# Two-layer diffusion backbone on one core: a PSUM bank for the last of seven products, and GpSimd's instructions in pieces of 256 columns

## Chip, cores and metric

The kernel runs on one core of a Trainium2 chip. The metric is the device time of one execution in microseconds (us); the kernel before took 1140.18 us, the median of three runs (1138.74 to 1141.05).

## What is computed

512 latent tokens of 1024 channels pass through two layers. Each layer is a normalisation with modulation, a mixer (layer 0: differential attention beside a long convolution; layer 1: a pooling mixer), a second normalisation, and a squared-ReLU MLP of width 4096; a last RMSNorm ends it. What matters here is the MLP and the normalisation ahead of it:

```python
h_lat = h_lat + mod_l[5] * _sq_relu_mlp(
    _modulate(_rmsnorm(h_lat, norm2_g[i]), mod_l[3], mod_l[4]), mlp_w1[i], mlp_w2[i])

def _sq_relu_mlp(h, w1, w2):
    return jnp.square(jax.nn.relu(h @ w1)) @ w2
```

## The kernel before

Channels lie on the 128 partitions, tokens (512) on the columns. All products are float32 made of two rounded parts: an operand is split into a high part (`hi`, ScalarE's cast, L163) and a remainder (`lo`, a subtraction on VectorE or GpSimd, L164), and a product is three matmuls, hi·hi, hi·lo and lo·hi. A weight tile is 128x1024 (eight blocks of 128x128). It is fetched by SyncE, cast by ScalarE (1024 columns) and its remainder is formed by VectorE or, in most tiles, by GpSimd (`split`, called by `wload` and `w_split`).

The instructions of every engine stand in the order in which the code is written (`tc.manual_schedule`), so an engine whose next instruction waits does nothing else.

An MLP goes through four blocks of 1024 hidden channels: first the eight tiles `f` of the block (h @ w1, ReLU, square), then eight tiles `r` (times w2), each added into the stream `h` by VectorE (`h_add`, L1569). In layer 1 the first product of blocks 1, 2 and 3 is made for two tiles `f` and two token halves at once with **seven products** in place of eight (`pair7`, Strassen's scheme in Winograd's form): four pairs per block, three blocks, so twelve pairs of seven products. A product is 12 matmuls of 256 columns: eight with `whi` (L1669, L1670), then four with `wlo` (L1672). In a pair:

- `w0` and `w1` are prepared during the pair before, `w2` and `w3` at its start. They are sums of two weight tiles a and b: GpSimd adds a and b into `scr` (L1444) and folds b (L1447), and splits `w3` and the next `w0` (L164); VectorE forms the sums in `scr` for the next `w1` (`pair_sums`, L1430, L1431) and the remainders of `w1` and `w2` (L164).
- The products go to three PSUM banks of 512 columns, two halves each: `px`, `py`, `pz`, from a ring of six. The seven in order: `px` left, `py` left, `py` right, `pz` right, `px` right, `py` left again, `pz` left.
- VectorE adds them up: L1731 (both halves of `py` + `p1`, 512 columns), then `pair_sums` for the next pair, then `u3` (L1738, reads `px` right) and `s1` right (L1739, reads `pz` right), L1742, and at the end L1746 (both halves of `pz` + `u3`, 512 columns). The last product overwrites `pz` left, while L1739 reads `pz` right: TensorE waits for L1739 ahead of it.
- `finish` (L1754 to L1758) squares on ScalarE and forms the remainder `gl` on VectorE (L1758), interleaved with the next pair through `before(0)`, `before(1)`, and so on.

In block 0 of layer 1's MLP, `act_sums` forms the sums of the activations that the seven products read (`th`): GpSimd L1647, L1648 and L164, VectorE L1649 to L1653.

At the end of an MLP or mixing stage, `residual_norm` mixes the last tiles `r` with the next normalisation: squares (`ssq`, VectorE L1522 or GpSimd), column sums on TensorE (`nt`, L1530), and `mod` with its two VectorE steps L1543 and L1556 per tile.

Of the kernel before, what the change touches and what calls it, by code (L numbers as in the profile page):

```python
# [9 lines left out]
F32 = mybir.dt.float32  # L10
F32R = mybir.dt.float32r
AF = mybir.ActivationFunctionType
ALU = mybir.AluOpType
# [5 lines left out]
P = 128  # L19
D = 1024  # L20
ND = 8
T = 512
# [71 lines left out]
def body(ctx: ExitStack, tc: tile.TileContext, I, out):  # L94
# [6 lines left out]
    def f32(ap):  # L101
        return ap.bitcast(F32)
# [46 lines left out]
    def nm(s):  # L149
        cnt[0] += 1  # L150
        return f"{s}_{cnt[0]}"
# [7 lines left out]
    def w_tile(name, dt=F32R):  # L159
        return keep.tile([P, T], dt, name=nm(name), tag="W", bufs=8)  # L160

    def split(hi, lo, src, lo_eng=None):
        act.copy(out=hi, in_=src)  # L163
        (lo_eng or dve).tensor_tensor(out=lo, in0=src, in1=f32(hi), op=ALU.subtract)  # L164

    streams = {"s": (st, "s", 4, 2, st)}

# [1256 lines left out]
    def pair_sums(k):  # L1424

        if k in sums_done or k not in pairs:
            return
        sums_done.add(k)
        a, b, t = wraw[k], wraw[k + 1], scr[0]
        dve.tensor_tensor(out=t[:, :T], in0=b[:, :T], in1=a[:, :T], op=ALU.add)  # L1430
        dve.tensor_tensor(out=t[:, T : 2 * T], in0=t[:, :T], in1=a[:, T:], op=ALU.add)  # L1431

    def s3_part(k):
        c = (2 + k // 2 % 2) * T
        return scr[0][:, c : c + T]

    def pair_first(k, n=2):

        if k not in pairs:
            return  # L1440
        a, b = wraw[k], wraw[k + 1]
        if (k, 1) not in first_done:
            first_done.add((k, 1))
            pool.tensor_tensor(out=s3_part(k), in0=a[:, :T], in1=b[:, :T], op=ALU.add)  # L1444
        if n == 2 and (k, 2) not in first_done:
            first_done.add((k, 2))
            pool.tensor_tensor(out=b[:, :T], in0=b[:, :T], in1=b[:, T:], op=ALU.add)  # L1447

    def w_prep(n):
        while len(wsp) < min(n, len(wsrc)):  # L1450
# [182 lines left out]
    def mlp(layer, ah_, al_, nrm, i_norm, shift_in, last_norm, mod_next, load=None, seven=True):  # L1633
# [10 lines left out]
        def act_sums(i):  # L1644
            b1, b2, t = (ml.tile([P, T], F32, name=nm("b"), tag="sq", bufs=3) for _ in range(3))
            x, y = slice(0, 256), slice(256, 512)
            pool.tensor_tensor(out=b1, in0=f32(ah_[i]), in1=f32(al_[i]), op=ALU.add)  # L1647
            pool.tensor_tensor(out=b2, in0=f32(ah_[i + 4]), in1=f32(al_[i + 4]), op=ALU.add)  # L1648
            dve.tensor_tensor(out=t[:, x], in0=b1[:, x], in1=b1[:, y], op=ALU.subtract)  # L1649
            dve.tensor_tensor(out=t[:, y], in0=b2[:, y], in1=b1[:, y], op=ALU.subtract)  # L1650
            yield
            dve.scalar_tensor_tensor(out=b1[:, y], in0=t[:, y], scalar=-1.0, in1=b1[:, x], op0=ALU.mult, op1=ALU.subtract)
            dve.scalar_tensor_tensor(out=b2[:, y], in0=b1[:, y], scalar=-1.0, in1=b2[:, x], op0=ALU.mult, op1=ALU.subtract)  # L1653
            split(th[:, i, 0, 0:2, :], th[:, i, 1, 0:2, :], t.rearrange("p (a t) -> p a t", a=2), pool)
            split(th[:, i, 0, 2, :], th[:, i, 1, 2, :], b1[:, y], pool)
            split(ah_[i][:, y], al_[i][:, y], b2[:, y], pool)
            yield
# [8 lines left out]
        def product(o, w, c, b):  # L1666
            for i in range(4):
                l = w[0][:, c + i * P : c + (i + 1) * P]
                pe.matmul(o, l, b[i][0], start=(i == 0), stop=False)  # L1669
                pe.matmul(o, l, b[i][1], start=False, stop=False)  # L1670
            for i in range(4):
                pe.matmul(o, w[1][:, c + i * P : c + (i + 1) * P], b[i][0], start=False, stop=(i == 3))  # L1672
        for blk in range(4):
# [35 lines left out]
            def pair7(f, before):  # L1709

                k = wk[0]
                wk[0] += 2
                w_fetch(k + 8)
                pair_first(k + 2, 1)
                w0, w1 = wsp[k], wsp[k + 1]
                w2 = w_split(k, wraw[k + 1], dve)
                w3 = w_split(k + 1, s3_part(k), pool, T)
                pair_first(k + 2)
                x, y = slice(0, 256), slice(256, 512)
                px, py, pz = ps_m("f"), ps_m("f"), ps_m("f")  # L1720
                small = [ml.tile([P, 256], F32, name=nm("na"), tag="na", bufs=4) for _ in range(2)]
                p1, u3 = small
                s1 = ml.tile([P, T], F32, name=nm("r"), tag="r", bufs=3)
                twice = lambda v: v.rearrange("p (a t) -> p a t", a=1).to_broadcast([P, 2, 256])
                both = lambda v: v.rearrange("p (a t) -> p a t", a=2)
                product(px[:, x], w0, 0, b_part(0, 0))
                act.copy(out=p1, in_=px[:, x])
                product(py[:, x], w0, T, b_part(1, 0))
                before(0)
                product(py[:, y], w1, 0, t_part(2))  # L1730
                dve.tensor_tensor(out=both(s1), in0=both(py), in1=twice(p1), op=ALU.add)  # L1731
                before(1)
                w_prep(k + 3)
                before(4)
                pair_sums(k + 2)
                product(pz[:, y], w2, 0, t_part(0))
                product(px[:, y], w3, 0, t_part(1))
                dve.tensor_tensor(out=u3, in0=px[:, y], in1=s1[:, y], op=ALU.add)  # L1738
                dve.tensor_tensor(out=s1[:, y], in0=pz[:, y], in1=s1[:, y], op=ALU.add)  # L1739
                before(2)  # L1740
                product(py[:, x], w1, T, b_part(1, 1))
                dve.tensor_tensor(out=s1[:, y], in0=py[:, x], in1=s1[:, y], op=ALU.add)  # L1742
                w_prep(k + 4)
                product(pz[:, x], w2, T, [(ah_[i][:, y], al_[i][:, y]) for i in range(4)])
                s2 = ml.tile([P, T], F32, name=nm("r"), tag="r", bufs=3)
                dve.tensor_tensor(out=both(s2), in0=both(pz), in1=twice(u3), op=ALU.add)  # L1746
                for u in range(2):
                    mk = att_tile if f + u < 4 else w_tile
                    gh[f + u], gl[f + u] = mk("gh"), mk("gl")

                def finish(part):
                    for u, s, sign in ((0, s1, 1.0), (1, s2, -1.0)):
                        if part in (4 * u, 3):
                            act.activation(out=s, in_=s, func=AF.Relu, scale=sign)  # L1754
                            act.activation(out=gh[f + u], in_=s, func=AF.Square)
                            act.activation(out=s, in_=s, func=AF.Square)
                        if part in (u + 1, 3):
                            dve.tensor_tensor(out=gl[f + u], in0=s, in1=f32(gh[f + u]), op=ALU.subtract)  # L1758

                return finish  # L1760
# [64 lines left out]


    n1 = Norm()
    dh, dl = nl_tiles()
    sh1 = mods[:, 0, 3, :]
    w_fetch(6)  # L1830
# [321 lines left out]
```

## Time and profile before

| what | value |
|---|---|
| median of three runs | 1140.18 us |
| the profiled execution | 1138.79 us |
| its span | 1137.0 us |
| mean granted TensorE clock | 0.983 of full speed |
| TensorE busy (matmul) | 1084.9 us, 95% |
| VectorE busy | 772.9 us, 68% |
| GpSimd busy | 490.4 us, 43% |
| ScalarE busy | 482.4 us, 42% |

TensorE carries the kernel, so time is lost where it stands idle or where its clock is low. VectorE and GpSimd are far from full on average, but their busy time contains waiting: an instruction that has started and can't go on counts as busy.

### The profile page before, as it was taken

The numbers are of one execution on the slowest core, as the hardware profiler recorded it, in microseconds if no ns is written. First come the engines' busy times: TensorE is split into PE (matmuls) and PEld (weight loads), VectorE is DVE, ScalarE is ACT, GpSimd is POOL, SyncE is SP. The second block draws the span as 40 slices with busy tenths as digits, with TensorE's granted clock in tenths as the row PEclk, the third lists the DMA queues.
The fourth block names the chain that finished last, engine by engine and source line by source line (L and its number), as shares of the span: only waits on it lengthen the run. The fifth ranks groups of instructions, "written<-read, shape, count | busy, mean of one in ns | idle before, by whom it ended". The sixth has DMA issues, their size and how long they took to land.

```text
span 1137.0 us, 15915 instructions
## 1 busy us (share of the span) xinstructions
PE 1084.9 (95%) x6172; PEld 937.1 (82%) x6172; DVE 772.9 (68%) x1114; ACT 482.4 (42%) x812; POOL 490.4 (43%) x364
## 2 busy tenths in 40 slices
PE   8899999999999999999999999899997998999896
PEld 5488988788989988888888889898877888989886
DVE  6679899999856646686676683765457627725744
ACT  4454356666453531331341232655324614714541
POOL 4447337885564222122122123463476435354412
PEclk9899999999999999999999999999998999999998
DMA  9786753225522346567557462112322322332202
GB/s 328 276 271 214 251 170 128 75 65 168 180 100 75 111 137 236 166 205 256 168 197 252 147 213 97 40 73 74 111 75 75 109 78 74 112 111 75 94 19 74
DMA packets 48654, 161.42 MB, mean 142 GB/s; under 512 B 5250, under 2 KB 8578, under 8 KB 48452
## 3 DMA queue, kind: packets, MB, share of 16 engines
q1 hardware_dynamic: 46132, 149.93, 39.0%
q0 software_dynamic: 2448, 10.49, 2.7%
q8 instruction: 48, 0.79, 0.3%
q14 instruction: 26, 0.21, 0.1%
HBM read 156.20 MB, written 4.20 MB: 141 GB/s over the span
## 4 chain that ended last, share of the span: by engine, by line
PE 71%; DVE 16%; issue 3%; ACT 3%; POOL 3%; DMA 3%; SPq 0%; POOLq 0%; DVEq 0%; ACTq 0%
PE r L197 11%; PE r L199 10%; PE r L203 10%; PE f L199 6%; PE f L203 6%; PE f L197 6%; PE f L1669 2%; DVE g L629 2%; PE f L1672 2%; PE f L1670 2%; DVE gl L1758 1%; PE v L878 1%; DVE nl L1556 1%; DVE scr L1430 1%; DMA g<-in_adaN 1%
## 5 line engine op out<-in xcount | busy, mean ns | idle before, releaser
L164 POOL TENSOR_TENSOR wlo<-raw,whi 128x1024 fp32r<-128x1024 f32 x77 | 190.7, 2479 | 367.5 <-ACT whi L163 312.9
L197 PE MATMUL r<-gh,whi 128*128 128x512 f32 (+1 forms) x576 | 207.3, 368 | 0.0
L199 PE MATMUL r<-gl,whi 128*128 128x512 f32 (+1 forms) x576 | 207.0, 368 | 0.0
L163 ACT CAST whi<-raw 128x1024 fp32r<-128x1024 f32 x135 | 139.7, 1043 | 137.3 <-PE r L199 102.1
L1569 DVE SCALAR_TENSOR_TENSOR h<-r,mods,h 128x512 f32<-128x512 f32 (+1 forms) x81 | 54.3, 671 | 149.0 <-PE r L203 148.8
L203 PE MATMUL r<-gh,wlo 128*128 128x512 f32 (+1 forms) x576 | 130.7, 368 | 0.0
L197 PEld LDWEIGHTS r<-gh,whi 128*128 128x128 f32 x576 | 108.3, 188 | 19.1
L199 PEld LDWEIGHTS r<-gl,whi 128*128 128x128 f32 x576 | 108.4, 188 | 18.9
L203 PEld LDWEIGHTS r<-gh,wlo 128*128 128x128 f32 x576 | 100.5, 188 | 18.9
L197 PE MATMUL f<-nh,whi 128*128 128x512 f32 (+1 forms) x320 | 116.0, 370 | 0.0
L199 PE MATMUL f<-nl,whi 128*128 128x512 f32 (+1 forms) x320 | 116.0, 370 | 0.0
L1498 DVE CUSTOM_DVE_ANT_0 g<-g,sbcl 128x1024 f32<-128x1024 f32 x48 | 105.2, 2191 | 0.0
L164 DVE TENSOR_TENSOR wlo<-raw,whi 128x1024 fp32r<-128x1024 f32 x58 | 76.5, 1319 | 12.0 <-ACT whi L163 12.0
L1687 DVE TENSOR_TENSOR r<-r 128x512 f32<-128x512 f32 (+1 forms) x48 | 37.6, 784 | 67.9 <-ACT gh L1686 67.8
L1685 ACT ACTIVATE r<-f 128x512 f32<-128x512 f32 (+1 forms) x48 | 25.1, 523 | 131.6 <-PE f L203 130.0
L203 PE MATMUL f<-nh,wlo 128*128 128x512 f32 (+1 forms) x320 | 73.1, 371 | 0.0
L199 PEld LDWEIGHTS f<-nl,whi 128*128 128x128 f32 x320 | 60.2, 188 | 10.8
L197 PEld LDWEIGHTS f<-nh,whi 128*128 128x128 f32 x320 | 60.2, 188 | 10.8
L1669 PE MATMUL f<-nh,whi 128*128 128x256 f32 x192 | 50.8, 296 | 16.2 <-DVE r L1739 16.2
L203 PEld LDWEIGHTS f<-nh,wlo 128*128 128x128 f32 x320 | 56.3, 188 | 10.8
L197 PE MATMUL u<-ah,whi 128*128 128x512 f32 x160 | 63.3, 395 | 0.7 <-ACT vh L889 0.7
L199 PE MATMUL u<-al,whi 128*128 128x512 f32 x160 | 62.5, 391 | 0.0
(413 smaller groups left out, 2525.3 us busy)
## 6 DMA issues: line engine op xcount, KB each, us to landing
raw<-in_w SPq DMA_DIRECT2D x128, 512.0 KB, 4.4
g<-in_adaT SPq DMA_DIRECT2D x80, 512.0 KB, 4.2
g<-in_adaN SPq DMA_DIRECT2D x16, 512.0 KB, 8.5
raw<-in_w_hy SPq DMA_DIRECT2D x12, 512.0 KB, 4.4
raw<-in_w_qk SPq DMA_DIRECT2D x8, 512.0 KB, 4.0
pth<-in_pth POOLq DMA_DIRECT2D x4, 768.0 KB, 6.8
raw<-in_w_out SPq DMA_DIRECT2D x5, 512.0 KB, 4.0
x<-in_xT SPq DMA_DIRECT2D x8, 256.0 KB, 7.3
```

The lines of the kernel that those rows point to most:

```text
L163: act.copy(out=hi, in_=src)
L164: (lo_eng or dve).tensor_tensor(out=lo, in0=src, in1=f32(hi), op=ALU.subtract)
L197: pe.matmul(ps, wh[:, c], ah[i][:, t0 : t0 + n], start=(i == 0), stop=False)
L199: pe.matmul(ps, wh[:, c], al[i][:, t0 : t0 + n], start=False, stop=False)
L203: pe.matmul(ps, wl[:, i * P : (i + 1) * P], ah[i][:, t0 : t0 + n], start=False, stop=(i == k - 1))
L629: dve.tensor_tensor_reduce(out=g, in0=g, in1=sbc[0], scale=1.0, scalar=0.0, op0=ALU.mult, op1=ALU.add, accum_out=mods[:, 0, 2 + k // ND, k ...
L1498: dve.tensor_tensor_reduce(out=gin[k], in0=gin[k], in1=sbc[0], scale=1.0, scalar=0.0, op0=ALU.mult, op1=ALU.add, accum_out=mods[:, layer, ...
L1569: dve.scalar_tensor_tensor(out=hs[d][:, seg], in0=pp[:, :n], scalar=gate[:, d : d + 1], in1=hs[d][:, seg], op0=ALU.mult, op1=ALU.add)
L1669: pe.matmul(o, l, b[i][0], start=(i == 0), stop=False)
L1670: pe.matmul(o, l, b[i][1], start=False, stop=False)
L1685: act.activation(out=r, in_=pp[:, :n], func=AF.Relu)
L1687: dve.tensor_tensor(out=r, in0=r, in1=r, op=ALU.mult)
```

## The change

A flag `pieces` is set ahead of the last five tiles of layer 0's output projection, in front of the first MLP. From there GpSimd's remainders (`split` with GpSimd) go in slices of 256 columns: 1024 columns as four instructions, 512 as two. L1444 and L1447 go in two slices each, and the 512-column split of `th` in `act_sums` becomes two splits of 256 (ScalarE's cast too). The 512-column sums L1647 and L1648 stay whole.

In `pair7` the last product has a bank `pw_` of its own, the fourth of the pair in the ring of six. The two 512-column additions become two of 256 each (seven additions of 256 columns per pair, before two of 512 and three of 256), a third small tile `u2` joins `p1` and `u3`, and `pair_sums` moves behind `s1` right, `u3` and `s2` right on VectorE.

```diff
+    pieces = [False]
+
     def split(hi, lo, src, lo_eng=None):
         act.copy(out=hi, in_=src)
-        (lo_eng or dve).tensor_tensor(out=lo, in0=src, in1=f32(hi), op=ALU.subtract)
+        if lo_eng is pool and pieces[0]:
+
+            w = src.shape[-1]
+            for c in range(0, w, 256):
+                r = slice(c, min(c + 256, w))
+                pool.tensor_tensor(out=lo[:, r], in0=src[:, r], in1=f32(hi)[:, r], op=ALU.subtract)
+        else:
+            (lo_eng or dve).tensor_tensor(out=lo, in0=src, in1=f32(hi), op=ALU.subtract)
...
-            pool.tensor_tensor(out=s3_part(k), in0=a[:, :T], in1=b[:, :T], op=ALU.add)
+            for r in (slice(0, 256), slice(256, T)):
+                pool.tensor_tensor(out=s3_part(k)[:, r], in0=a[:, r], in1=b[:, r], op=ALU.add)
...
                 product(py[:, y], w1, 0, t_part(2))
-                dve.tensor_tensor(out=both(s1), in0=both(py), in1=twice(p1), op=ALU.add)
+                dve.tensor_tensor(out=s1[:, x], in0=py[:, x], in1=p1, op=ALU.add)
+                dve.tensor_tensor(out=u2, in0=py[:, y], in1=p1, op=ALU.add)
                 before(1)
                 w_prep(k + 3)
                 before(4)
+                product(pz[:, y], w2, 0, t_part(0))
+                dve.tensor_tensor(out=s1[:, y], in0=pz[:, y], in1=u2, op=ALU.add)
+                product(px[:, y], w3, 0, t_part(1))
+                dve.tensor_tensor(out=u3, in0=px[:, y], in1=u2, op=ALU.add)
+                s2 = ml.tile([P, T], F32, name=nm("r"), tag="r", bufs=3)
+                dve.tensor_tensor(out=s2[:, y], in0=pz[:, y], in1=u3, op=ALU.add)
                 pair_sums(k + 2)
-                product(pz[:, y], w2, 0, t_part(0))
-                product(px[:, y], w3, 0, t_part(1))
-                dve.tensor_tensor(out=u3, in0=px[:, y], in1=s1[:, y], op=ALU.add)
-                dve.tensor_tensor(out=s1[:, y], in0=pz[:, y], in1=s1[:, y], op=ALU.add)
                 before(2)
                 product(py[:, x], w1, T, b_part(1, 1))
                 dve.tensor_tensor(out=s1[:, y], in0=py[:, x], in1=s1[:, y], op=ALU.add)
                 w_prep(k + 4)
-                product(pz[:, x], w2, T, [(ah_[i][:, y], al_[i][:, y]) for i in range(4)])
-                s2 = ml.tile([P, T], F32, name=nm("r"), tag="r", bufs=3)
-                dve.tensor_tensor(out=both(s2), in0=both(pz), in1=twice(u3), op=ALU.add)
+                pw_ = ps_m("f")
+                product(pw_[:, x], w2, T, [(ah_[i][:, y], al_[i][:, y]) for i in range(4)])
+                dve.tensor_tensor(out=s2[:, x], in0=pw_[:, x], in1=u3, op=ALU.add)
...
     n1 = Norm()
+    pieces[0] = True
```

On TensorE, block 2's second pair, the end of the sixth product (into `py`) and the start of the seventh. Before, the seventh goes to `f_8885`, which is `pz`, and waits for VectorE:

```order
L1672 MATMUL f_8884<-nh_7055,wlo_8848 128x256
L1672 MATMUL f_8884<-nh_7056,wlo_8848 128x256
L1672 MATMUL f_8884<-nh_7057,wlo_8848 128x256
L1669 MATMUL f_8885<-nh_7050,whi_8874 128x256 [waits DVE_49]
L1670 MATMUL f_8885<-nl_7058,whi_8874 128x256
L1669 MATMUL f_8885<-nh_7051,whi_8874 128x256
```

Now it goes to `f_9228`, the new bank, and nothing is waited for:

```order
L1686 MATMUL f_9121<-nh_7190,wlo_9082 128x256
L1686 MATMUL f_9121<-nh_7191,wlo_9082 128x256
L1686 MATMUL f_9121<-nh_7192,wlo_9082 128x256
L1683 MATMUL f_9228<-nh_7185,whi_9109 128x256
L1684 MATMUL f_9228<-nl_7193,whi_9109 128x256
L1683 MATMUL f_9228<-nh_7186,whi_9109 128x256
```

The wait of TensorE's queue on VectorE ahead of the seventh product is gone. On VectorE, the same pair. Before:

```order
L1731 TENSOR_TENSOR r_8888<-f_8884,na_8886 128x512 [waits PE_49,Activation_49]
L1758 TENSOR_TENSOR gl_8866<-r_8763,gh_8865 128x512 [waits DVE_49,Activation_49]
L1430 TENSOR_TENSOR scr_7169<-raw_8710,raw_8676 128x512 [waits DMAHW5_49,DMAHW6_49,DVE_49,Pool_49]
L1431 TENSOR_TENSOR scr_7169<-scr_7169,raw_8676 128x512 [waits DVE_49]
L1738 TENSOR_TENSOR na_8887<-f_8883,r_8888 128x256 [waits PE_49]
L1739 TENSOR_TENSOR r_8888<-f_8885,r_8888 128x256 [waits DVE_49]
L1758 TENSOR_TENSOR gl_8868<-r_8863,gh_8867 128x512 [waits Activation_49]
L1742 TENSOR_TENSOR r_8888<-f_8884,r_8888 128x256 [waits DVE_49,PE_49]
L164 TENSOR_TENSOR wlo_8981<-scr_7169,whi_8980 128x1024 [waits Activation_49]
L1746 TENSOR_TENSOR r_8996<-f_8885,na_8887 128x512 [waits PE_49]
```

Now (L1439 and L1440 are `pair_sums`, L1772 is `gl`, L173 the remainder of the next `w1`):

```order
L1742 TENSOR_TENSOR r_9126<-f_9121,na_9123 128x256 [waits PE_49,Activation_49]
L1743 TENSOR_TENSOR na_9124<-f_9121,na_9123 128x256
L1772 TENSOR_TENSOR gl_9100<-r_8991,gh_9099 128x512 [waits DVE_49,Activation_49]
L1748 TENSOR_TENSOR r_9126<-f_9122,na_9124 128x256 [waits DVE_49,PE_49]
L1750 TENSOR_TENSOR na_9125<-f_9120,na_9124 128x256 [waits PE_49]
L1752 TENSOR_TENSOR r_9206<-f_9122,na_9125 128x256 [waits DVE_49]
L1439 TENSOR_TENSOR scr_7304<-raw_8934,raw_8895 128x512 [waits DMAHW6_49,DMAHW5_49,Pool_49]
L1440 TENSOR_TENSOR scr_7304<-scr_7304,raw_8895 128x512 [waits DVE_49]
L1772 TENSOR_TENSOR gl_9102<-r_9064,gh_9101 128x512 [waits Activation_49]
L1756 TENSOR_TENSOR r_9126<-f_9121,r_9126 128x256 [waits PE_49]
L173 TENSOR_TENSOR wlo_9225<-scr_7304,whi_9224 128x1024 [waits Activation_49]
L1760 TENSOR_TENSOR r_9206<-f_9228,na_9125 128x256 [waits PE_49]
```

The two instructions of `pair_sums` now stand behind the three additions that read PSUM, and so behind the fifth product of the pair.

## Rows read from the trace of the kernel before

**Rows 1.** The page, parts 1 and 5: busy us and share; a group's busy us, mean ns.
```profile
PE 1084.9 (95%) x6172; PEld 937.1 (82%) x6172; DVE 772.9 (68%) x1114; ACT 482.4 (42%) x812; POOL 490.4 (43%) x364
...
L163 ACT CAST whi<-raw 128x1024 fp32r<-128x1024 f32 x135 | 139.7, 1043 | 137.3 <-PE r L199 102.1
```
**Rows 2.** Waits: engine, line, awaited engine and line: us in total, times, longest.
```profile
PEld f L1669 <- DVE r L1739: 18.6, 12, 4.1
PE f L1669 <- DVE r L1739: 16.2, 9, 3.9
PE nt L1530 <- DVE ssq L1522: 3.8, 2, 2.5
```
**Rows 3.** Timeline, second pair of block 2: TensorE; columns start us, duration us, instruction, [idle before].
```profile
956.12 0.64 PE L1672 MATMUL f<-nh,wlo 128*128 128x256 f32 x4
...
961.79 0.63 PE L1672 MATMUL f<-th,wlo 128*128 128x256 f32 x4
963.21 0.64 PE L1672 MATMUL f<-nh,wlo 128*128 128x256 f32 x4
966.29 0.39 PE L1669 MATMUL f<-nh,whi 128*128 128x256 f32 x1 [2.44 <-DVE r L1739]
```
**Rows 4.** Timeline, the same pair: VectorE.
```profile
960.30 2.71 DVE L1758 TENSOR_TENSOR gl<-r,gh 128x512 fp32r<-128x512 f32 x1
962.94 1.77 DVE L1430 TENSOR_TENSOR scr<-raw,raw 128x512 f32<-128x512 f32 x1
964.75 0.69 DVE L1431 TENSOR_TENSOR scr<-scr,raw 128x512 f32<-128x512 f32 x1
965.36 0.42 DVE L1738 TENSOR_TENSOR na<-f,r 128x256 f32<-128x256 f32 x1
965.81 0.42 DVE L1739 TENSOR_TENSOR r<-f,r 128x256 f32<-128x256 f32 x1
...
967.08 1.22 DVE L164 TENSOR_TENSOR wlo<-scr,whi 128x1024 fp32r<-128x1024 f32 x1
```
**Rows 5.** Timeline, the same pair: GpSimd.
```profile
958.38 1.29 POOL L1447 TENSOR_TENSOR raw<-raw 128x512 f32<-128x512 f32 x1
960.05 2.42 POOL L164 TENSOR_TENSOR wlo<-raw,whi 128x1024 fp32r<-128x1024 f32 x1 [0.38 <-ACT whi L163]
962.43 1.73 POOL L1444 TENSOR_TENSOR scr<-raw,raw 128x512 f32<-128x512 f32 x1
```
**Rows 6.** Groups by line and shape, GpSimd: busy us, mean ns, idle before us.
```profile
L164 POOL TENSOR_TENSOR wlo<-raw,whi 128x1024 fp32r<-128x1024 f32 x77 | 190.7, 2479 | 367.5 <-ACT whi L163 312.9 <-PE r L203 54.6
```
**Rows 7.** Timeline, the kernel's end: three GpSimd instructions of 256 columns back to back.
```profile
1130.35 2.09 POOL L1974 TENSOR_TENSOR o<-hm,nbs 128x256 f32<-128x256 f32 x3 [1.23 <-ACT nbs L1969]
```
**Rows 8.** Windows: stretch, length, busy us of PE, PEld, DVE, ACT, POOL; granted clock, DMA, GB/s.
```profile
862.00:866.00 4.00, 3.02 (x14) 3.02 (x15) 2.50 (x6) 1.91 (x2) 0.00 (x0) 0.57 0.67 231
1057.00:1060.50 3.50, 3.50 (x19) 3.50 (x19) 2.40 (x3) 2.02 (x4) 1.90 (x1) 0.52 0.64 257
...
726.00:729.50 3.50, 3.50 (x18) 3.50 (x18) 0.60 (x3) 0.69 (x2) 0.70 (x1) 0.51 0.02 5
364.20:367.60 3.40, 3.40 (x18) 3.40 (x18) 0.65 (x2) 1.88 (x2) 2.52 (x2) 0.51 0.00 0
```
**Rows 9.** Timeline, end of layer 0's MLP: GpSimd, VectorE and TensorE.
```profile
716.83 2.24 DVE L1556 SCALAR_TENSOR_TENSOR nl<-na,mods,nh 128x256 fp32r<-128x256 f32 x1
...
720.12 0.47 DVE L1556 SCALAR_TENSOR_TENSOR nl<-na,mods,nh 128x256 fp32r<-128x256 f32 x1
...
721.34 2.36 POOL L164 TENSOR_TENSOR wlo<-raw,whi 128x1024 fp32r<-128x1024 f32 x1 [2.54 <-ACT whi L163]
721.70 2.27 DVE L1556 SCALAR_TENSOR_TENSOR nl<-na,mods,nh 128x256 fp32r<-128x256 f32 x1 [0.71 <-ACT nh L1551]
...
724.46 0.35 PE L1530 MATMUL nt<-sil,ssq 128*128 128x1 f32 x2 [2.52 <-DVE ssq L1522]
```
**Rows 10.** Timeline, start of block 1 of layer 1's MLP: TensorE.
```profile
851.43 0.38 PE L1669 MATMUL f<-th,whi 128*128 128x256 f32 x1 [2.18 <-ACT th L163]
```

More of the change, by code (lines that the diff above doesn't have):

```diff
@@ L1443, in pair_first @@
             first_done.add((k, 1))
-            pool.tensor_tensor(out=s3_part(k), in0=a[:, :T], in1=b[:, :T], op=ALU.add)
+            for r in (slice(0, 256), slice(256, T)):
+                pool.tensor_tensor(out=s3_part(k)[:, r], in0=a[:, r], in1=b[:, r], op=ALU.add)
         if n == 2 and (k, 2) not in first_done:
             first_done.add((k, 2))
-            pool.tensor_tensor(out=b[:, :T], in0=b[:, :T], in1=b[:, T:], op=ALU.add)
+            for c in (0, 256):
+                pool.tensor_tensor(
+                    out=b[:, c : c + 256], in0=b[:, c : c + 256], in1=b[:, T + c : T + c + 256], op=ALU.add
+                )
     def w_prep(n):
@@ L1653, in act_sums @@
             dve.scalar_tensor_tensor(out=b2[:, y], in0=b1[:, y], scalar=-1.0, in1=b2[:, x], op0=ALU.mult, op1=ALU.subtract)
-            split(th[:, i, 0, 0:2, :], th[:, i, 1, 0:2, :], t.rearrange("p (a t) -> p a t", a=2), pool)
+            for n in range(2):
+                split(th[:, i, 0, n, :], th[:, i, 1, n, :], t[:, n * 256 : (n + 1) * 256], pool)
             split(th[:, i, 0, 2, :], th[:, i, 1, 2, :], b1[:, y], pool)
@@ L1720, in pair7 @@
                 px, py, pz = ps_m("f"), ps_m("f"), ps_m("f")
-                small = [ml.tile([P, 256], F32, name=nm("na"), tag="na", bufs=4) for _ in range(2)]
-                p1, u3 = small
+                p1, u2, u3 = (ml.tile([P, 256], F32, name=nm("na"), tag="na", bufs=4) for _ in range(3))
                 s1 = ml.tile([P, T], F32, name=nm("r"), tag="r", bufs=3)
-                twice = lambda v: v.rearrange("p (a t) -> p a t", a=1).to_broadcast([P, 2, 256])
-                both = lambda v: v.rearrange("p (a t) -> p a t", a=2)
                 product(px[:, x], w0, 0, b_part(0, 0))
```

## The prediction

> **What bounds the kernel now.** I read the engines' busy time first: TensorE is busy 95% of the span, nobody else over 70% [rows 1], so what counts is where TensorE waits or runs slow. The list of waits comes next. From the start of the first MLP on, one entry stands out: the seventh product of a pair waits for VectorE's L1739, in all 16.2 us of idle matmul time and 18.6 us of idle weight loads, for twelve pairs [rows 2]. The second entry is 3.8 us ahead of the column sums of two normalisations [rows 2].
>
> The timeline of one pair shows why. The fifth product's last four matmuls run to 961.79 + 0.63 = 962.42 and the sixth's to 963.85; the seventh starts at 966.29 [rows 3]. VectorE has the additions L1738 and L1739, which need only the fifth product, behind three other instructions. The remainder `gl` takes 2.71 us, the first sum 1.77, the second 0.69, and L1739 ends at 966.23 [rows 4]. The same shape of instruction takes 0.69 us when nothing disturbs it [rows 4]. GpSimd tells the rest: its 1024-column remainder runs 960.05 to 962.47, and `gl`, begun at 960.30, ends at 963.01, 0.54 us after it. GpSimd's next, 512 columns, begun at 962.43, takes 1.73 where its like took 1.29, and ends 1.15 us after `gl`; the first sum, begun at 962.94, ends 0.55 us after that [rows 4, 5]. So the two engines take turns, instruction by instruction, in whatever reads two operands from SBUF, and the long one makes the short one wait. The additions from PSUM (L1738, 0.42) show no such wait. The Trainium skill says the same ("SBUF — State Buffer", Who interferes with whom: a VectorE instruction with two SBUF inputs and a GpSimd one that reads SBUF exclude each other for a whole instruction); the trace agrees, with 2.71 us for 0.69.
>
> The normalisation ahead of layer 1 shows it again: a VectorE step of 0.47 us takes 2.24 and 2.27 us, the second time beside a GpSimd remainder of 2.36 us that began 0.36 us earlier, and TensorE then waits 2.52 us for VectorE [rows 9].
>
> **The change part by part.** All terms are against the profiled execution, 1138.8 us; gains have a minus.
>
> *The bank.* The changed order has no wait ahead of the seventh product. The idle time there goes: between 16.2 and 18.6 us [rows 2]. Matmuls overlap a little where nothing waits, and that overlap returns too, so I take **-18**.
>
> *The clock after those waits.* After two of them the granted clock stood at its lower level, 1.2 GHz: 4.0 us at a mean of 0.57 and 3.5 us at 0.52 of full speed [rows 8], which is 4.0 x 0.43 + 3.5 x 0.48 = 3.4 us of lost speed, part of the first inside the wait itself. If TensorE no longer stops there, I expect no fall there: **-3.0** (0 to -3.4).
>
> *`pair_sums` moved back.* It feeds the next pair's `w1`, so the question is what is late next. Take the pair of the rows without TensorE's wait. Products end every (961.79 - 956.12)/4 = 1.42 us [rows 3], the seventh would follow the sixth at about 963.7, and the next pair's third product, the first user of `w1`, starts three later, at 963.7 + 3 x 1.42 = 967.9, and its low parts are needed at 968.9. The fifth product is done at 962.42; three additions of 0.42 bring VectorE to 963.8. Each sum now waits for at most one GpSimd piece, about 0.7, and takes 0.55 after it: 965.0 and 966.3. ScalarE's cast of 1.04 us [rows 1] gives the high part at 967.4, 0.5 us early. `gl` runs beside the cast, and VectorE's remainder of 1.22 us [rows 4] gives the low part at 968.7 to 969.4, from 0.2 early to 0.5 late. It fits, with little to spare.
>
> *The turns as a budget.* In one block GpSimd has 36 pieces (six each of L1444 and L1447, eight for `w3`, 16 for the 1024-column remainders), and VectorE eight remainders of 1024 and twelve instructions of 512 columns with two SBUF operands. A piece counts between 1.15/2 = 0.57 us (what 512 columns took after VectorE let go) and 0.73 (three in a row take 2.09, so 0.70 each, and the last of a row a little more [rows 7]). VectorE's count 1.22 and 0.55 to 0.69 [rows 4]. The sum is 36 x 0.57 + 9.8 + 6.6 = 36.9 us at the low end and 36 x 0.73 + 9.8 + 8.3 = 44.4 at the high one, against 28 x 1.42 = 39.8 us of products. So the cover is thin: nothing is lost at the low end, 4.6 us per block at the high one. I take the low end as the nearer, since the measured turns overlap at their ends, and put **+1.0 per block, +3** in all (0 to +13.8), for waits that appear at the next pair's weights and at the hand-over to the tiles `r`, where the last `gl` now ends later against TensorE.
>
> *GpSimd's own length.* 77 remainders of 1024 columns become four pieces each: 4 x 0.68 = 2.7 us for 2.4, and 40 instructions of 512 become two. That is some 30 us more GpSimd time in a span where it is 43% busy [rows 1]. Nearly all of it hides: those tiles are prepared two products `r` ahead, and GpSimd stands idle 368 us in front of them [rows 6]. If that cover were gone, it would cost TensorE 0.3 us per tile. It shows in one place, the start of block 1, where `act_sums` stands behind L1444, L1447 and a 1024-column remainder on GpSimd and TensorE then waits 2.18 us for `th` [rows 10]: **+0.8** (0.3 to 1.2). The two casts of `th` in place of one lie in that term.
>
> *VectorE's seven additions.* 7 x 0.42 against 2 x 0.69 + 3 x 0.42 is 0.3 us more per pair, in time that VectorE has; the fourth tile of the bank ring and the third small tile are released a pair earlier than they are asked for. Nothing.
>
> *The normalisations.* At the end of layer 0's mixing and of its MLP, two VectorE steps each stand 1.8 us too long behind a GpSimd remainder [rows 9]. In pieces each waits at most some 0.7, so VectorE is about 1.1 earlier twice over, 2.2 us in all, and of the 3.8 us of TensorE's wait [rows 2] (1.3 and 2.52) 1.2 and 2.1 go: **-3.3** (-2.0 to -3.8). After both, the clock was low for 3.5 us at 0.51 and 3.4 at 0.51 [rows 8], 1.7 us each. A short wait for ScalarE's square stays, so I count one of the two: **-1.7** (0 to -3.4).
>
> Sum: -18 - 3.0 + 3 + 0.8 - 3.3 - 1.7 = -22.2, so 1138.8 - 22.2 = 1116.6 us. The profiled execution lies 1.4 us under the median of the runs, at their lower edge (1138.74 to 1141.05), so I forecast **1117** for the median.
>
> **The rivals.**
> 1. *The turns are too many* (high end of the budget). The waits go from the seventh product to the next pair's first and third, at 4.6 us per block in place of 1.0. For it: the budget's high end passes the products, and `pair_sums` starts later. Against it: GpSimd's last pair in a block is light, and a measured turn is short. Time: 1117 + 3 x 3.6 = 1128.
> 2. *Slower: GpSimd's pieces set the pace.* Splitting doesn't lessen what the two engines must do one after the other, and each piece adds its own start. A block with seven products takes 39.8 + 16.2/3 = 45.2 us now. With h us per piece the budget is 36h + 18.1, and it passes 45.2 at h = 0.75, and eats the 5 us of the normalisations too above h = 0.80. The point that decides is a piece above 0.80 us. At h = 0.90 it is 50.5 us, 5.3 more per block, less 5: 1140 + 16 - 5 = 1151. Against it: alone, 256 columns take 0.70 [rows 7]. The rule of the Trainium skill named above ("SBUF — State Buffer", Who interferes with whom) speaks for this rival: whole instructions exclude each other, so by it alone pieces move waits about and make no room. The trace agrees with the exclusion in each turn above, with its 0.54 and 0.55 us.
> 3. *The bank is not the wait.* Then only the normalisations gain, 5 us less 0.8: 1136. Against it: the changed order shows the seventh product with no wait at all.
>
> **How the numbers follow.** Forecast 0.74, rival 1 0.17, rival 2 0.05, rival 3 0.04. The best bounds together give 1138.8 - 18.6 - 3.4 + 0.3 - 3.8 - 3.4 = 1110; upward the range takes in rival 1, to 1129. A measurement of this kernel tells 0.2% (2.3 us) from no change. Faster by more than that are the forecast, rival 1 and most of rival 3: 0.92; within it 0.03; slower 0.05.
>
> **What would show it.** Right: no wait on VectorE ahead of the seventh product; pairs of 9.9 us (7 x 1.42); no instruction of `gl` or of the sums above some 1.4 us; GpSimd's pieces at 0.7 to 0.85; full clock through blocks 2 and 3; TensorE's wait ahead of L1530 under 1 us. Rival 1 would show as waits on `whi` or `wlo` at the next pair's first, third or fourth product. The prediction is wrong if TensorE still waits over 5 us in the three blocks beyond the start of block 1, or if GpSimd's pieces run one after another while VectorE stands.

## The result and the profile after

| kernel | median (runs) | ratio to before, 95% interval |
|---|---|---|
| before | 1140.62 us (4: 1138.74 to 1143.05) | |
| changed | 1110.73 us (4: 1110.01 to 1111.55) | 0.974 [0.972, 0.976] |

The changed kernel is 29.9 us faster; 23 were forecast. The time lies in the range, near its fast end. Its profiled execution took 1111.55 us with a span of 1109.6, 27.4 us under the span before.

Page of the changed kernel, parts 1 and 5, which answers to [rows 1] and [rows 6]:

```profile
PE 1076.8 (97%) x6172; PEld 931.1 (84%) x6172; DVE 716.5 (65%) x1138; ACT 480.7 (43%) x816; POOL 581.1 (52%) x635
...
L171 POOL TENSOR_TENSOR wlo<-raw,whi 128x256 fp32r<-128x256 f32 x308 | 271.2, 913 | 296.1 <-ACT whi L165 257.0
```

GpSimd is 90.7 us busier and VectorE 56.4 us less, though VectorE has 24 instructions more: what VectorE lost was waiting inside its instructions. TensorE has the same number of matmuls and is busy 8.1 us less; a matmul at the low clock counts longer.

Waits of TensorE in the changed kernel (engine, line, awaited engine and line: us in total, times, longest), which answer to [rows 2]:

```profile
PE f L1683 <- ACT th L165: 2.3, 1, 2.3
...
PE nt L1543 <- ACT sq L1531: 1.7, 3, 0.9
...
PE f L1686 <- POOL wlo L171: 0.5, 1, 0.5
...
PE f L1683 <- ACT whi L165: 0.5, 1, 0.5
...
PE f L1684 <- POOL th L171: 0.4, 1, 0.4
PE nt L1543 <- DVE ssq L1535: 0.3, 1, 0.3
```

The entry of 16.2 us is gone, and the 3.8 us ahead of the column sums are 0.3. The largest entry left in the MLP is the wait for `th` at the start of block 1, 2.3 us, which was there before.

Timeline, second pair of block 2, VectorE in the changed kernel (start, duration, instruction), which answers to [rows 4]:

```profile
947.23 1.25 DVE L1439 TENSOR_TENSOR scr<-raw,raw 128x512 f32<-128x512 f32 x1
948.51 1.11 DVE L1440 TENSOR_TENSOR scr<-scr,raw 128x512 f32<-128x512 f32 x1
949.55 1.22 DVE L1772 TENSOR_TENSOR gl<-r,gh 128x512 fp32r<-128x512 f32 x1
950.69 0.41 DVE L1756 TENSOR_TENSOR r<-f,r 128x256 f32<-128x256 f32 x1
951.03 1.43 DVE L173 TENSOR_TENSOR wlo<-scr,whi 128x1024 fp32r<-128x1024 f32 x1
```

The same stretch, GpSimd, which answers to [rows 5]:

```profile
945.80 3.28 POOL L171 TENSOR_TENSOR wlo<-raw,whi 128x256 fp32r<-128x256 f32 x4
949.03 2.34 POOL L1454 TENSOR_TENSOR scr<-raw,raw 128x256 f32<-128x256 f32 x2
```

`gl` beside GpSimd takes 1.22 us where [rows 4] have 2.71; GpSimd's pieces take 3.28/4 = 0.82 and 2.34/2 = 1.17 each there, against 0.70 back to back [rows 7]. The engines still take turns, but what VectorE waits in one, 1.22 - 0.69 = 0.53 us, is now under the length of one 256-column piece. The sums and `gl` stay below the 1.4 us that the prediction set as their mark: in the three blocks the longest `gl` takes 1.27 us and the longest sum 1.25. GpSimd's pieces don't keep theirs, 0.7 to 0.85 us: the 308 of the page have a mean of 0.913, because they wait in the turns too.

Windows of the changed kernel (length, busy us of PE, PEld, DVE, ACT, POOL; granted clock, DMA share, GB/s): the place of the first clock fall of before [rows 8], the start of block 1, and blocks 2 and 3 of the seven products:

```profile
364.20:367.60 3.40, 3.40 (x31) 3.40 (x30) 2.86 (x7) 2.52 (x7) 3.40 (x5) 1.00 0.01 2
846.20:849.70 3.50, 3.34 (x15) 3.34 (x16) 2.49 (x3) 2.45 (x4) 3.50 (x5) 0.51 0.00 0
929.30:968.90 39.60, 39.60 (x337) 39.60 (x336) 31.60 (x48) 24.98 (x38) 32.05 (x34) 1.00 0.26 92
1013.20:1052.90 39.70, 39.70 (x337) 39.70 (x336) 31.59 (x48) 24.75 (x37) 31.57 (x34) 1.00 0.28 94
```

Blocks 2 and 3 run without any gap at 2.4 GHz. The clock stood at its lower level only once in the stretch from the first normalisation to the end of the MLP's blocks, behind the wait for `th`: the granted clock is 1.00 from 364.2 to 846.2 and from 849.7 to 1053.0.

The time by place, from the starts of the matmuls in the timelines. A block here runs from the start of its first product to the start of the matmul that follows its 28th. In the changed kernel block 2 goes from 929.23 to 968.98, before from 944.36 to 989.56.

| stretch | before | after | difference |
|---|---|---|---|
| all ahead of block 1's first pair | 845.40 | 838.77 | -6.63 |
| block 1 of seven products | 54.78 | 46.28 | -8.50 |
| block 2 | 45.20 | 39.75 | -5.45 |
| block 3 | 46.38 | 39.74 | -6.64 |

The four make 27.2 of the 27.4 us of the spans. The 6.6 us ahead of block 1 lie at the two normalisations: the same matmul starts at 359.85 before and 359.71 after ahead of the first, at 367.58 and 364.43 behind it, and at 729.32 and 722.48 behind the second. Their waits for VectorE fell by 3.8 - 0.3 = 3.5 us, and both clock falls of [rows 8] that followed them are gone, 1.7 us each, 3.4: together 6.9, with the 6.6 measured.

### The profile page after: what moved, and what is told of

It is laid out like the page before. It is cut to its first block, busy times and chain, and to the rows that moved or that the text cites. A ratio compares the mean times of both kernels' runs of the same rounds, so it can differ in the third digit from the quotient of the medians.

```text
span 1109.6 us, 16252 instructions
## 1 busy us (share of the span) xinstructions
PE 1076.8 (97%) x6172; PEld 931.1 (84%) x6172; DVE 716.5 (65%) x1138; ACT 480.7 (43%) x816; POOL 581.1 (52%) x635
## 5 line engine op out<-in xcount | busy, mean ns | idle before, releaser
L171 POOL TENSOR_TENSOR wlo<-raw,whi 128x256 fp32r<-128x256 f32 x308 | 271.2, 913 | 296.1 <-ACT whi L165 257.0
L1701 DVE TENSOR_TENSOR r<-r 128x512 f32<-128x512 f32 (+1 forms) x48 | 32.0, 667 | 81.2 <-ACT gh L1700 81.1
L173 DVE TENSOR_TENSOR wlo<-raw,whi 128x1024 fp32r<-128x1024 f32 x58 | 73.7, 1271 | 10.9 <-ACT whi L165 10.9
L1511 DVE CUSTOM_DVE_ANT_0 g<-g,sbcl 128x1024 f32<-128x1024 f32 x48 | 65.3, 1361 | 0.0
L734 POOL TENSOR_TENSOR wlo<-raw,whi 128x1024 fp32r<-128x1024 f32 x17 | 42.5, 2501 | 37.4 <-ACT whi L725 25.0
```

Of the source, the lines that this page charges most:

```text
L171: pool.tensor_tensor(out=lo[:, r], in0=src[:, r], in1=f32(hi)[:, r], op=ALU.subtract)
L734: ew(pool if k else dve).tensor_tensor(out=wts[k][1], in0=raws[k], in1=f32(wts[k][0]), op=ALU.subtract)
L1511: dve.tensor_tensor_reduce(out=gin[k], in0=gin[k], in1=sbc[0], scale=1.0, scalar=0.0, op0=ALU.mult, op1=ALU.add, accum_out=mods[:, layer, ...
```

## The experiments

Two things in the changed kernel could make it faster: what was done to the pairs (a bank and an order), and the pieces. The first four runs take them apart. All have the time of before from the same chip beside them: 1140.79 us in the first four, 1140.08 in the next four, 1140.05 and 1140.47 in the last two.

**Bank and order alone, GpSimd whole**

```diff
-    pieces[0] = True
...
-            for r in (slice(0, 256), slice(256, T)):
-                pool.tensor_tensor(out=s3_part(k)[:, r], in0=a[:, r], in1=b[:, r], op=ALU.add)
+            pool.tensor_tensor(out=s3_part(k), in0=a[:, :T], in1=b[:, :T], op=ALU.add)
```

(L1458 and the split of `th` likewise.)

> The bank of its own and the new order of VectorE's additions stay; GpSimd's instructions are whole again (1024 and 512 columns). Theory: in the pairs TensorE waits for nothing long even beside whole GpSimd instructions, because the additions it depends on stand ahead of the sums; the pieces earn their share at the two normalisations, 6.6 us between the two traces (TensorE reached the first pair at 838.8 us in place of 845.4). So 1110.7 + 6.6 - 0.6 (shorter start of block 1) = about 1117 us, 1115 to 1121; no fall of the clock in blocks 2 and 3. Rival, the pieces are needed in the pairs too: the two sums behind a whole instruction come 1 to 2 us late for the next pair's third product, in nine pairs, and the time is about 1128 us.

Measured: 1119.40 us (1116.27 to 1123.92), ratio 0.982 [0.979, 0.985]. The blocks take 47.32, 40.02 and 40.04 us: bank and order alone leave 1.6 us in all of what the pieces would give there. The medians lie 8.7 us and the two spans 8.3 us above the changed kernel; 6.3 of the 8.3 lie ahead of block 1, at the normalisations, whose wait is back. The kernel's waits of TensorE:

```profile
PE nt L1539 <- DVE ssq L1531: 3.7, 2, 2.5
```

Windows of the same kernel, behind the two normalisations:

```profile
363.90:367.40 3.50, 3.50 (x19) 3.50 (x18) 0.64 (x2) 1.90 (x3) 2.59 (x2) 0.51 0.00 0
725.80:729.30 3.50, 3.50 (x18) 3.50 (x18) 0.61 (x4) 0.59 (x1) 0.70 (x1) 0.52 0.02 5
```

Both falls of the clock are back with it.

**Pieces alone, the pair as before**

```diff
+                dve.tensor_tensor(out=both(s1), in0=both(py), in1=twice(p1), op=ALU.add)
+                pair_sums(k + 2)
...
-                pw_ = ps_m("f")
-                product(pw_[:, x], w2, T, [(ah_[i][:, y], al_[i][:, y]) for i in range(4)])
+                product(pz[:, x], w2, T, [(ah_[i][:, y], al_[i][:, y]) for i in range(4)])
```

> GpSimd in pieces, the pair as before (shared bank, old order). Theory: the normalisations keep their 6.6 us; the seventh product still waits for L1739, which stands behind one remainder and two sums, but each of these now waits for at most one piece (about 1.1 to 1.2 us each in place of 2.7, 1.8 and 0.7): a wait of 0.5 to 1.2 us in each of twelve pairs, so 1110.7 + 6 to 12 = 1117 to 1123 us. Rival, the bank alone carries the product stages: the waits stay at some 16 us and the time is about 1131 us.

Measured: 1118.09 us (1115.14 to 1120.18), ratio 0.981 [0.978, 0.984]. The wait ahead of the seventh product is still there, at a third of the 16.2 us of [rows 2]:

```profile
PE f L1683 <- DVE r L1753: 5.2, 7, 2.5
```

The blocks take 50.94, 41.16 and 41.14 us, so pieces alone leave 7.5 us in the blocks. The normalisations are as in the changed kernel, with no fall of the clock. Each half of the change thus brings some 22 us by itself and both together 30: they overlap on the same wait. In the three blocks, where both together bring 20.6 us, bank and order alone bring 19.0 and pieces alone 13.1; the gain at the normalisations comes with the pieces. Shorter pieces let VectorE reach L1739's addition (L1753 here) earlier; bank and order make it unnecessary to be early.

**Pieces and bank, `pair_sums` in its old place**

```diff
                 dve.tensor_tensor(out=u2, in0=py[:, y], in1=p1, op=ALU.add)
+                pair_sums(k + 2)
...
                 dve.tensor_tensor(out=s2[:, y], in0=pz[:, y], in1=u3, op=ALU.add)
-                pair_sums(k + 2)
```

> As the changed kernel, but the two sums for the next pair stand where they stood before, ahead of the additions. Theory: with a bank of its own the seventh product waits for no addition, so the place of the sums is free: 1110 to 1112 us, no wait ahead of the seventh product. Rival, the order did it: the waits come back and the time is 1117 us or more.

Measured: 1109.87 us (1108.80 to 1112.77), ratio 0.973 [0.971, 0.976]; blocks 46.80, 39.70, 39.70, and no wait ahead of the seventh product. The rival falls: the order isn't needed here.

**Pieces and order, the seventh product in `pz`**

```diff
-                pw_ = ps_m("f")
-                product(pw_[:, x], w2, T, [(ah_[i][:, y], al_[i][:, y]) for i in range(4)])
-                dve.tensor_tensor(out=s2[:, x], in0=pw_[:, x], in1=u3, op=ALU.add)
+                product(pz[:, x], w2, T, [(ah_[i][:, y], al_[i][:, y]) for i in range(4)])
+                dve.tensor_tensor(out=s2[:, x], in0=pz[:, x], in1=u3, op=ALU.add)
```

> As the changed kernel, but the last product goes to the left half of pz again. Theory: with the sums moved back, the last reader of pz (the right half of s2) is done some 0.9 us after the fifth product, before TensorE gets to the seventh, so the shared bank costs at most 0.1 to 0.3 us per pair: 1111 to 1114 us. Rival, the bank did it: waits as before return, a good 1 us in each of twelve pairs, 1123 us or more.

Measured: 1109.31 us (1107.63 to 1111.20), ratio 0.973 [0.970, 0.976]; blocks 46.38, 39.75, 39.75. The rival falls: with the sums behind the additions, the reader of `pz` is done in time and no bank of its own is needed. With the run before it: given the pieces, either the bank or the order removes the wait, and the other adds nothing that these runs can tell. Which of the two did it with whole instructions wasn't tried.

**Pieces of 512 columns**

```diff
-            for c in range(0, w, 256):
-                r = slice(c, min(c + 256, w))
+            for c in range(0, w, 512):
+                r = slice(c, min(c + 512, w))
```

> Edit: the changed kernel with GpSimd's remainders in pieces of 512 columns in place of 256, L1454 and L1458 whole (512). Theory (the two engines take turns instruction by instruction, so VectorE's wait is the length of GpSimd's instruction): gl and the sums beside GpSimd take 1.15 + 0.55 = 1.7 us in place of 1.1 to 1.25, a normalisation step up to 1.2 + 0.47 = 1.7 in place of 0.95; TensorE's wait at the normalisations comes back in part (about half of the 3.7 us with whole instructions, 1.5 to 2.5, and with it one or two of the two clock falls of 1.7). Blocks 2 and 3 stay within 0.3 us of 39.75. Time 1112 to 1116. Rival (what a piece costs is its start, so that fewer, longer pieces are better, and the wait has little to do with length): 1110 or less, waits at the normalisations as now.

Measured: 1118.51 us (1116.57 to 1119.05), ratio 0.980 [0.975, 0.985]: above both ranges, about as with whole instructions. The blocks did as expected (40.03 twice). The normalisations lost not half of the gain but all of it. The kernel's waits of TensorE:

```profile
PE nt L1539 <- DVE ssq L1531: 3.7, 2, 2.5
```

VectorE at the second normalisation in this kernel, and TensorE's wait behind it (timeline):

```profile
716.38 1.14 DVE L1565 SCALAR_TENSOR_TENSOR nl<-na,mods,nh 128x256 fp32r<-128x256 f32 x1
717.43 1.51 DVE L1531 TENSOR_TENSOR ssq<-ssq,sq 128x256 f32<-128x256 f32 x1
...
721.24 1.20 DVE L1565 SCALAR_TENSOR_TENSOR nl<-na,mods,nh 128x256 fp32r<-128x256 f32 x1 [0.72 <-ACT nh L1560]
722.36 1.48 DVE L1531 TENSOR_TENSOR ssq<-ssq,sq 128x256 f32<-128x256 f32 x1
...
723.98 0.35 PE L1539 MATMUL nt<-sil,ssq 128*128 128x1 f32 x2 [2.50 <-DVE ssq L1531]
```

And the same place in the changed kernel:

```profile
713.64 0.57 DVE L1569 SCALAR_TENSOR_TENSOR nl<-na,mods,nh 128x256 fp32r<-128x256 f32 x1
714.14 0.95 DVE L1535 TENSOR_TENSOR ssq<-ssq,sq 128x256 f32<-128x256 f32 x1
...
715.79 0.87 DVE L1569 SCALAR_TENSOR_TENSOR nl<-na,mods,nh 128x256 fp32r<-128x256 f32 x1
...
717.38 0.66 DVE L1569 SCALAR_TENSOR_TENSOR nl<-na,mods,nh 128x256 fp32r<-128x256 f32 x1 [0.33 <-ACT nh L1564]
717.96 0.96 DVE L1535 TENSOR_TENSOR ssq<-ssq,sq 128x256 f32<-128x256 f32 x1
...
719.07 0.35 PE L1543 MATMUL nt<-sil,ssq 128*128 128x1 f32 x2 [0.32 <-DVE ssq L1535]
```

Undisturbed these steps take 0.47 and 0.42 us. With 512 columns four instructions each wait once, for 0.67 + 1.09 + 0.73 + 1.06 = 3.55 us; with 1024 columns two waited 1.8 each, 3.6 [rows 9]. Halving a piece made each wait shorter and doubled the number of waits. With 256 columns the five above lose 0.10 + 0.53 + 0.40 + 0.19 + 0.54 = 1.76 us. VectorE also stands idle for ScalarE's `nh` on the way, 0.71 us before, 0.72 with 512 columns and 0.33 with 256: together 4.28, 4.27 and 2.09 us. TensorE's wait follows it: 2.52, 2.50 and 0.32 us. The length of one turn was expected rightly; that the waits would sum to half was not.

**Pieces of 128 columns**

```diff
-            for c in range(0, w, 256):
-                r = slice(c, min(c + 256, w))
+            for c in range(0, w, 128):
+                r = slice(c, min(c + 128, w))
```

(L1454 and L1458 in four slices each.)

> Edit: the changed kernel with GpSimd's instructions in pieces of 128 columns. From 0.70, 1.29 and 2.40 us for 256, 512 and 1024 columns a piece of 128 alone would take about 0.41 (0.12 of it a fixed start). Theory (a turn is as long as the instruction, with a small start): VectorE's instructions beside GpSimd drop to 0.9 to 1.0 us, GpSimd's part of the turns per block is 72 x 0.3 to 0.41 = 22 to 30 us, plus VectorE's 16 to 18, 38 to 48 against 39.75: blocks 2 and 3 between 39.75 and 42; the start of block 1 0.5 later. Time 1110 to 1116. Rival (every piece costs a whole turn of some 0.55 us whatever its width, since VectorE is let in after each): 72 x 0.55 + 17 = 57 us per block, 15 more than now or more, time 1140 to 1160.

Measured: 1132.32 us (1128.39 to 1133.89), ratio 0.993 [0.991, 0.995]; blocks 57.78, 43.84, 44.18: between the two theories. Timeline of GpSimd in this kernel, block 2:

```profile
967.19 1.72 POOL L1454 TENSOR_TENSOR scr<-raw,raw 128x128 f32<-128x128 f32 x4
```

Windows of the same kernel, block 2:

```profile
942.90:986.80 43.90, 41.09 (x337) 40.05 (x337) 30.43 (x48) 25.29 (x38) 39.68 (x68) 1.00 0.27 88
```

A piece takes 1.72/4 = 0.43 us alone, as expected, so the rival's fixed turn is wrong. But GpSimd is busy 39.68 of 43.90 us, where the changed kernel has 32.05 of 39.60, and VectorE gains little (the mean of the 24 `gl` goes from 0.95 to 0.80 us). GpSimd's own pace becomes the limit: waits for `wlo` from GpSimd of 6.2 us and for `whi` of 4.6 come up. The theory's mechanism stands and its size doesn't: blocks 2 and 3 are 2 us above its 42. Block 1 lost 11.5 us against the changed kernel. In it the clock stood at 1.2 GHz for 6.9, 3.4 and 3.4 us (granted 0.51, 0.50 and 0.50 from 849.2, 866.3 and 890.2 us), in the changed kernel once for 3.4; 10.3 us more at half speed are at most 5.1 of the 11.5, by estimate. The rest wasn't taken apart.

**More additions, and more fills: is there a budget of turns?**

```diff
+            more = ml.tile([P, 256], F32, name=nm("more"), tag="more")
...
                 w_prep(k + 3)
+                for c in range(4):
+                    pool.tensor_tensor(out=more, in0=f32(ah_[c])[:, x], in1=f32(al_[c])[:, x], op=ALU.add)
```

The second kernel has `pool.memset(more, 0.0)` in place of the addition.

> Edit: the changed kernel with four more GpSimd additions of 256 columns per pair, two operands from SBUF, whose result nothing uses; 16 pieces more per block (36 become 52). Theory (turns are a budget against the products): 52 x 0.57 to 0.59 + 15.3 to 18 = 45 to 49 us per block against 39.75, so blocks 1 to 3 lengthen by 4 to 9 us each: time 1122 to 1135, with waits for whi or wlo at the next pairs' first products. Rival (the cover is ample, because VectorE's two-operand instructions fall only beside a part of the pieces and the rest run at GpSimd's own 0.70 us): GpSimd's own 52 x 0.70 = 36 us still fits into 39.75, and the blocks lengthen by at most 1 us each, time 1110 to 1114.

> Edit: the changed kernel with four GpSimd fills of 256 columns per pair into a tile that nothing uses, at the place of the four additions of the run before; they read nothing. Theory (only what reads two operands from SBUF takes turns with VectorE): VectorE is not kept waiting by them, and they cost GpSimd's own time alone; the blocks lengthen by less than a third of what the additions cost, time 1110 to 1114. Rival (any GpSimd instruction takes a turn): as with the additions, within 2 us of their time.

Measured: with additions 1131.18 us (1129.75 to 1132.43), ratio 0.992 [0.989, 0.995]; with fills 1113.43 us (1111.10 to 1114.06), ratio 0.976 [0.972, 0.980], each in the range of its theory. The blocks are 54.55, 45.32, 45.43 against 47.18, 39.98, 39.98. Windows of the kernel with additions, block 2:

```profile
937.70:983.00 45.30, 42.05 (x337) 41.25 (x336) 31.70 (x48) 24.69 (x37) 44.29 (x47) 0.96 0.23 83
```

Its waits of TensorE:

```profile
PE f L1687 <- POOL wlo L171: 12.6, 13, 2.6
```

GpSimd is busy 44.29 of 45.30 us and sets the pace. Groups by line and shape, from 838 to 1060 us, in the kernel with additions (busy us, mean ns, idle before; 40 of the 48 additions fall in it):

```profile
L1748 POOL TENSOR_TENSOR more<-nh,nl 128x256 f32<-128x256 f32 x40 | 47.5, 1186 | 2.4
```

The same view of the kernel with fills:

```profile
L1748 POOL MEMSET more<- 128x256 f32 x48 | 15.0, 313 | 2.1
```

An addition that reads two operands takes 1.19 us in this place, 0.49 more than the 0.70 that 256 columns take back to back [rows 7]; a fill, which reads nothing, 0.31. The Trainium skill's rule ("SBUF — State Buffer", Who interferes with whom: a whole instruction at a time) agrees with the additions, 0.70 us alone and 1.19 here. The timeline of the kernel with fills shows that these take no turn. GpSimd and VectorE, first pair of block 1:

```profile
857.00 1.43 POOL L1748 MEMSET more<- 128x256 f32 x4
856.95 1.23 DVE L173 TENSOR_TENSOR wlo<-scr,whi 128x1024 fp32r<-128x1024 f32 x1 [0.86 <-ACT whi L165]
```

Three of the four fills start and end while VectorE's remainder, with two operands from SBUF, is running; it takes 1.23 us, as in [rows 4], and all 48 fills lie between 0.304 and 0.318 us. The fills are also shorter by themselves, and how much of their small cost is owed to that wasn't separated. The budget is shown too: 16 more two-operand pieces per block, 13 of which start inside block 2's stretch, cost 5.6 us in a block that had no wait. Part of it is a fall of the clock (0.96 in the window); block 3, in which the clock didn't fall, lost 5.7.

**The sums for `th` earlier**

```diff
                 for d in range(ND):
                     if seven and blk == 0 and d % 2 == 0:
                         sums_ = act_sums(d // 2)
+                    if seven and blk == 0:
+                        next(sums_)
                     w = w_next()
...
-                    if seven and blk == 0:
-                        next(sums_)
```

> Edit: the changed kernel with each step of act_sums issued one place earlier in the code of block 0 (ahead of the weight preparation beside it in place of behind it), so that GpSimd's two 512-column sums stand ahead of L1454, L1458 and a remainder's pieces. Theory (the start of block 1 is late because act_sums stands behind GpSimd's pieces): TensorE's wait for th (2.3 us) goes, most of the 0.4 and 0.5 behind it, and the clock fall at 846 (1.7 us): block 1 takes 41 to 42 us in place of 46.28, time 1105 to 1107. Rival (th comes late for another reason, or the weights w0 and w1 of block 1, which are now formed later, are what TensorE then waits for): block 1 stays at 45 us or more, the wait moves from th to whi or wlo, time 1109 to 1112.

Measured: 1104.57 us (1103.58 to 1106.63), ratio 0.969 [0.967, 0.971], just under the theory's 1105: faster than the changed kernel by some 6 us, with no run of the one inside the range of the other. GpSimd ahead of block 1 in the changed kernel (timeline):

```profile
833.75 2.84 POOL L171 TENSOR_TENSOR wlo<-raw,whi 128x256 fp32r<-128x256 f32 x4
836.54 1.31 POOL L1660 TENSOR_TENSOR b<-nh,nl 128x512 f32<-128x512 f32 x1
837.78 1.32 POOL L1661 TENSOR_TENSOR b<-nh,nl 128x512 f32<-128x512 f32 x1
```

And in this kernel:

```profile
827.99 1.29 POOL L1660 TENSOR_TENSOR b<-nh,nl 128x512 f32<-128x512 f32 x1
829.24 1.29 POOL L1661 TENSOR_TENSOR b<-nh,nl 128x512 f32<-128x512 f32 x1
```

The sums end 8.6 us earlier, and no wait for `th` is left. Windows of this kernel, block 1:

```profile
838.20:879.50 41.30, 40.43 (x337) 39.82 (x336) 34.91 (x49) 26.38 (x40) 39.44 (x40) 1.00 0.31 103
```

Block 1 takes 41.46 us in place of 46.28 and stays at full clock. GpSimd is busy 39.44 of 41.30 us in it, so it has no room to spare there; the 1.7 us that block 1 still takes over the other blocks weren't taken apart.

**Pieces only around the normalisations**

```diff
+    pieces[0] = False
     mlp(1, dh2, dl2, n3, 3, sh3, n4, lambda: final(0, 256))
```

(L1454 and L1458 whole.)

> Edit: the changed kernel with GpSimd's pieces only up to the start of layer 1's MLP (so around the two normalisations), and whole instructions in the MLP with the seven products, where bank and order stay as changed. Theory (with bank and order in place, the pieces pay at the normalisations and hardly in the blocks of seven products): the blocks as in the run with bank and order alone (47.32, 40.02, 40.04, in all 1.6 us over the changed kernel), the normalisations as in the changed kernel (wait of 0.3 us for VectorE, full clock after them), time 1110.5 to 1114. Rival (the 8.7 us between the changed kernel and the one with whole instructions come from the MLP's r stages, where whole remainders delay VectorE, and not from the normalisations): 1116 to 1119.

Measured: 1112.46 us (1109.65 to 1114.47), ratio 0.975 [0.972, 0.978]; blocks 47.53, 40.04, 40.04. Its waits of TensorE:

```profile
PE nt L1539 <- DVE ssq L1531: 0.3, 1, 0.3
```

The rival falls. Beside bank and order, the pieces pay around the two normalisations and for 1.8 us in the blocks.

## Why the prediction was right, step by step

- **The mechanism** held: no wait ahead of the seventh product, blocks at 28 x 1.42 us, GpSimd and VectorE in turns of about 1.2 us. Rival 3 (the bank is not the wait) falls with the result; rival 1 with blocks 2 and 3, which have no gap. Rival 2's argument that pieces make no room is answered by pieces alone, which gained 22.7 us; its pace does exist: 16 more pieces, or pieces of 128 columns, bring it out. At 36 pieces of 256 in block 1 (34 in blocks 2 and 3) it isn't reached.
- **Bank and clock**, -18 and -3.0. Over the 39.74 us of a block with no gap, the three blocks before have 27.14 us more, of which 4.96 belong to the start of block 1: 22.2 us. After, 1.1 us is left, in block 1 alone (the waits of the next point). So 21.0 forecast as a gain, at most 22.2 measured: right. But the cause is wider than the text had it: given the pieces, either the moved sums or the bank is enough, and I priced the sum of all three as the bank's.
- **Waits that re-appear**, +3, 1.0 per block. This is the term that was mis-sized: blocks 2 and 3 have none, block 1 has 1.0 us (0.2 and 0.8, in the fifth products of its second and third pair, ahead of the matmuls with the `wlo` that GpSimd forms). "A sum waits for at most one piece" held (1.25 and 1.11 us), and the budget's low end, 36.9 us under 39.8, was the better reading than the 1.0 per block that I added to it; the additional pieces show that the margin is under 16 pieces.
- **Start of block 1**, +0.8: the waits there, with the clock fall behind them, grew from 4.96 to 5.46 us, +0.5.
- **The normalisations**, -3.3 idle and -1.7 clock. Idle -3.5: right, and VectorE came 2.2 us earlier at the second, as forecast, though only 1.8 of it in the turns and 0.4 in the wait for `nh`. Clock: both falls went, -3.4. The waits that stay are 0.40 us for ScalarE at both and 0.32 for VectorE at the second, and behind them the clock stayed at 2.4 GHz. I had counted one fall as lasting because a short wait was left; this is the other mis-sized term, -1.7.
- **GpSimd's own length**, nothing but in block 1: right, but by more cover than was counted on. Some 30 us more GpSimd time were forecast, at 0.68 us a piece; it is 90.7 us, at 0.913, because the pieces wait for VectorE as well. The sum had priced that time at nothing, so the miss didn't reach the forecast.

By the spans: -22.2 + 1.1 + 0.5 - 6.6 = -27.2 of 27.4 us measured, against -22.2 forecast. Of the 5.0 between them, 1.9 are the waits that didn't re-appear, 1.6 lie at the normalisations, 1.2 at bank and clock and 0.3 at the start of block 1. The medians are 29.9 apart: the profiled execution of before is 1.8 under its median, that of the changed kernel 0.8 over its own.

## What to carry to other kernels

Where two engines take turns in what they read from SBUF, try several widths of the longer engine's instruction: here 256 columns gained, 512 were as bad as 1024 at the normalisations, and 128 made so many turns that GpSimd set the pace. Count the turns of a stage against its time before splitting further, since a margin that shows no wait may be under 16 pieces of a block. And when a product waits for a reader of its buffer, moving other work behind that reader can be as good as a new buffer (shown here with the pieces in place); ask first what stands ahead of the reader in its queue.

## What was not expected of the hardware

VectorE's L1511 (L1498 before), which is not part of the change, became shorter with the pieces. Groups by line, before:

```profile
L1498 DVE CUSTOM_DVE_ANT_0 g<-g,sbcl 128x1024 f32<-128x1024 f32 x48 | 105.2, 2191 | 0.0
```

The changed kernel:

```profile
L1511 DVE CUSTOM_DVE_ANT_0 g<-g,sbcl 128x1024 f32<-128x1024 f32 x48 | 65.3, 1361 | 0.0
```

With bank and order alone its mean is 2190 ns, with pieces alone 1362, with pieces of 512 columns 1638 and with 128 it is 1326. It lost 40 us of busy time, most of what VectorE lost in all; no wait of TensorE names it.

The lower clock doesn't follow the length of a wait alone. Before, a window of the second pair of block 2, behind the wait of 2.44 us [rows 3], is at full clock:

```profile
966.00:970.00 4.00, 3.71 (x31) 3.71 (x32) 4.00 (x6) 2.74 (x5) 0.77 (x1) 1.00 0.67 266
```

At the first normalisation of before the clock fell to 0.51 [rows 8] behind waits of 1.25 and 0.40 us. What tells the two apart was not tried.
